# A differential-attention output projection in seven half-sized products, inside a decoder layer

## The chip, the cores and the metric

The kernel runs on one core of a Trainium2 chip, in one launch. The metric is the device time of one execution in microseconds, the median of several runs. All data are float32. The core's engines, as the profile names them: PE is TensorE (matmuls; PEld its weight loads), DVE is VectorE, ACT is ScalarE, POOL is GpSimd, and SP is the engine that only issues transfers here.

## The reference

One decoder layer for 512 tokens of width 1024. One combined input projection feeds three attention branches and three gates; each branch is projected to 1024 columns, the three are merged by sigmoid gates, projected again, added to the residual and normalised. Then follow an MLP of width 4096 with a squared ReLU, a gated per-layer embedding, and a second normalisation.

```python
proj = x @ w_in                                   # 512 x 1024 @ 1024 x 10752
(da_q, da_k, da_v, sb_q, sb_k, sb_v, dl_q, dl_k, dl_v, gates) = split(proj)
o_da = diff_attention(da_q, da_k, da_v, ...)      # 512 x 512, differential
o_sb = stick_breaking_attention(sb_q, sb_k, sb_v) # 512 x 512
o_dl = dilated_attention(dl_q, dl_k, dl_v, ...)   # 512 x 512
g = sigmoid(gates).reshape(B, S, 3, 1024)
merged = (g[:, :, 0] * (o_da @ w_branch_da) + g[:, :, 1] * (o_sb @ w_branch_sb)
          + g[:, :, 2] * (o_dl @ w_branch_dil))
x = layer_norm(alpha * x + merged @ w_out)
hid = relu(x @ w_up)
c = square(hid) @ w_down
ple = sigmoid(x @ w_ple_gate) * (p @ w_ple)
x = layer_norm(alpha * x + c + ple)
```

## The kernel before

Every large matmul is done in three passes. An operand `a` is split into a rounded part `h` (a cast on ScalarE) and a rest `l` (a subtraction on VectorE), and the product is `h*h + h*l + l*h`. Weights come in chunks of 128 x 1024 (512 KB): SP loads a chunk into one of seven raw tiles (`fill`, L182), ScalarE casts it to `wh` (L212), VectorE subtracts to `wl` (L214), and both live in rings of six. `pump` issues these splits as the chunks six places ahead are released.

The kernel is a list of items, executed in order. An item has a `mm` function that issues its matmuls into a PSUM bank (`mm_bank`, two, or `at_bank`, six), an `ev` function that evicts the bank and is issued at the next item, and optionally a `pre` function. Beside the items run generators, advanced by `step()` once or twice an item: the attention heads, and in `pending` other helpers. The tile framework orders the instructions of each engine when the program is built, so an engine's order need not be the source order.

Several products are already done in seven half-sized ones: with both matrices cut in 2 x 2 blocks, seven block products (called 2, 1, 7, 6, 4, 5, 3 in their order) of sums and differences of blocks give what eight would. This is so for the values of the dilated branch, the three gates (`seven`, used by `gate_alone` and `gate_chain`), the gate of the per-layer embedding, and the MLP. Sums of activation blocks (the "forms") are made on VectorE. Sums of weight blocks (`vsum`, `msum`, `gsum`, `usum`, `dsum`) are made by transfers on POOL's queue, from memory to memory with addition (`sum_steps`, L985 and L987): eight steps for each four sums. `credit` in the main loop grows by an item's size times its rate, and a step is issued for each whole unit; each step waits for a recent weight split.

The stages in order: the input projections with the attention heads between them, the stick-breaking branch (`branch_items(1)`), its gate, a second gate, the dilated branch, the third gate, the differential branch (`branch_items(0)`), the output projection (`wout_items`), the per-layer embedding, the MLP, and the last normalisation.

The differential branch before: `split_oT(0)` splits four tiles of 128 x 512 (attention output, transposed). For each half of the 1024 columns and each of four token tiles an item does 4 x 3 matmuls of 128 x 512 (L648 to L650). Its eviction multiplies the gate by the bank (L659) and adds it to `merged` (L660). A gate's sigmoid is made in place ahead of its item (`gate_sig`, L501). Behind each of the last four items stands a `turn_item(k)`: four transposes of 128 x 128 (L676), one column block of `merged` for all 512 tokens, split into `mh` and `ml` (L680, L681). The other four column blocks are turned among the first items of the output projection, whose first column half is therefore cut: all token tiles do the first four blocks of the inner dimension, then all do the last four (L766 to L770, evicted at L784).

Of the kernel before, what the change touches and what calls it, by code (L numbers as in the profile page):

```python
# [18 lines left out]
P = 128  # L19
# [36 lines left out]
def trunk(tc, a, out):  # L56
    nc = tc.nc
    es = ExitStack()
    with es:
# [14 lines left out]
        def slot(name, dt=F32):  # L74
            return big.tile([P, 512], dt, name=nm(name), tag="s", bufs=NSLOT)
# [7 lines left out]
        def at_bank():  # L83
            return psum.tile([P, 512], F32, name=nm("at"), tag="at", bufs=6)
# [67 lines left out]
        def chunk(src, w):  # L152
            return chunk_of(load(src, w))
# [78 lines left out]
        def item(cs, mm, ev, need=None, bank=None, size=1.0):  # L232
            items.append({"c": cs, "mm": mm, "ev": ev, "need": need, "bank": bank, "size": size})
# [403 lines left out]
        def branch_items(i, behind=()):  # L637
            behind = list(behind)
            for half in range(2):
                cs = [chunk(a["wb"][i, half, c].rearrange("p k n -> p (k n)"), 1024) for c in range(2)]  # L640
                for tt in range(4):
                    def mm(ps, tt=tt, cs=cs):
                        q = slice(tt * P, tt * P + P)
                        for k in range(4):
                            c = cs[k // 2]
                            n = slice(k % 2 * 512, k % 2 * 512 + 512)
                            h, lo = oTs[4 * i + k]
                            nc.tensor.matmul(ps, h[:, q], c["h"][:, n], start=k == 0, stop=False)  # L648
                            nc.tensor.matmul(ps, h[:, q], c["l"][:, n], start=False, stop=False)
                            nc.tensor.matmul(ps, lo[:, q], c["h"][:, n], start=False, stop=k == 3)  # L650

                    def ev(ps, tt=tt, half=half):
                        if i == 1:
                            t = slot("b1")
                            nc.scalar.copy(t, ps)
                            merged[tt, half] = t
                            return
                        g = sg.pop((i, tt, half))
                        nc.vector.tensor_mul(g, g, ps)  # L659
                        nc.vector.tensor_add(merged[tt, half], merged[tt, half], g)  # L660
# [7 lines left out]
                    if half and behind:  # L668
                        behind.pop(0)()

        merged_T = {}

        def turn_item(k):
            def mm(ps):
                for tt in range(4):
                    nc.tensor.transpose(ps[:, tt * P:tt * P + P], merged[tt, k // 4][:, k % 4 * P:k % 4 * P + P], ident)  # L676

            def ev(ps):
                h, lo = slot("mh", F32R), slot("ml", F32R)
                nc.scalar.copy(h, ps)  # L680
                nc.vector.tensor_sub(lo, ps, h.bitcast(F32))  # L681
                merged_T[k] = (h, lo)
            item([], mm, ev, size=0.08)

        last_plain = len(items)
        for it in items:
            it.setdefault("rate", 2.5)
        def first_gate(tt, half):
            g = gate_sig(1, tt, half)
            nc.vector.tensor_mul(merged[tt, half], merged[tt, half], g)  # L690
# [5 lines left out]
        for n, i in ((1, 2), (2, 0)):  # L696
            gate_chain(n, i)
            if n == 1:
                for j, th in enumerate([(tt, half) for half in range(2) for tt in range(4)]):
                    items[gated_at + 2 + j]["pre"] = lambda th=th: first_gate(*th)  # L700
            branch_at[i] = len(items)
            branch_items(i, () if i else [lambda k=k: turn_item(k) for k in range(4)])

        raws = {}
        forms = {}
# [46 lines left out]
        ln2_at = [None]  # L752

        def wout_items():
            kept = {}
            for half in range(2):
                cs = [chunk(a["wo"][half, c].rearrange("p k n -> p (k n)"), 1024) for c in range(4)]

                def part(tt, ks, last, half=half, cs=cs):
                    def mm(ps):  # L760
                        for k in ks:
                            c = cs[k // 2]
                            s = slice((k % 2) * 512, (k % 2) * 512 + 512)
                            h, lo = merged_T[k]
                            q = slice(tt * P, tt * P + P)
                            nc.tensor.matmul(ps, h[:, q], c["h"][:, s], start=k == 0, stop=False,  # L766
                                             skip_group_check=True)
                            nc.tensor.matmul(ps, h[:, q], c["l"][:, s], start=False, stop=False,
                                             skip_group_check=True)
                            nc.tensor.matmul(ps, lo[:, q], c["h"][:, s], start=False, stop=k == 7,  # L770
                                             skip_group_check=True)

                    def bank():
                        if ks[0] == 0:
                            kept[tt, half] = at_bank()
                        return kept[tt, half]

                    def ev(ps):
                        if ks[-1] != 7:
                            return  # L780
# [9 lines left out]
                    need = [cs[c] for c in sorted({k // 2 for k in ks})]  # L790
                    item(need if last else [], mm, ev, need=need, bank=bank, size=len(ks) / 8)
                if half:
                    for tt in range(4):
                        part(tt, range(8), tt == 3)
                    continue
                for tt in range(4):
                    part(tt, range(4), tt == 3)
                    for k in {1: (4, 5), 2: (6, 7)}.get(tt, ()):
                        turn_item(k)
                for tt in range(4):  # L800
                    part(tt, range(4, 8), tt == 3)

        def ln1_gen(tt):
            def fin(h, t):
# [153 lines left out]
        def sum_steps():  # L958
# [883 lines left out]
        for n, it in enumerate(items):  # L1842
# [5 lines left out]
                while active or waiting:  # L1848
                    step()
            for i in range(3):  # L1850
                if n == branch_at[i] - 2:
                    while any(k not in ready for k in range(4 * i, 4 * i + 4)):
                        step()
                    split_oT(i)
# [105 lines left out]
def _layout(x, p, w_in, da_lambda, da_norm, w_branch_da, w_branch_sb, w_branch_dil, w_out, ln1_g, ln1_b,  # L1960
# [17 lines left out]
    def quarters(w):  # L1978
# [8 lines left out]
        "wt": c(np.stack(tiles[2:])),  # L1987
        "wv": c(np.stack(vs)),

        "wb": c(np.stack([token_major(w[0]) for w in (w_branch_da, w_branch_sb, w_branch_dil)])),  # L1990
# [34 lines left out]
```

## The time and the profile before

| | |
|---|---|
| runs | 1054.17 us median (1053.24 to 1054.87, three runs) |
| the profiled execution | 1053.95 us, span 1052.0 us |
| granted clock of TensorE | 0.997 |
| gate items' end, differential branch, output projection | 585.4 to 601.7, 601.7 to 625.4, 625.4 to about 670 us of the span |

The span runs from the first to the last instruction of the profiled execution. In a row of a timeline the first number is the start, the second the duration, and the bracket, where there is one, the idle time before it with what ended it. In a row of the groups, the total busy time and the mean duration in ns stand behind the first bar and the idle time before them behind the second. In the table of stretches each engine has its busy time and, behind an x, its instructions.

### The profile page before, as it was taken

What the parts mean: (1) busy time and instruction counts of PE and PEld (TensorE: products, weight loads), DVE (VectorE), ACT (ScalarE), POOL (GpSimd) and SP (SyncE); (2) the same over time, 40 slices, a digit from 0 to 9 for tenths busy, and PEclk for the clock granted to TensorE, in tenths of its full rate; (3) what the DMA queues carried; (4) which work ended last, traced back from release to release, by engine and by line L of the source; (5) the groups of instructions that cost most, each with busy time, mean ns of one, the idle gap of its engine ahead of it and who ended that gap; (6) DMA issues with size and microseconds to landing.
All of it is one profiled execution on the core that took longest, in us unless ns stands there. A gap on an engine that the chain in (4) does not pass through costs nothing.

```text
span 1052.0 us, 15035 instructions
## 1 busy us (share of the span) xinstructions
PE 1037.5 (99%) x5474; PEld 883.7 (84%) x5474; DVE 763.5 (73%) x1356; ACT 582.9 (55%) x990; POOL 177.7 (17%) x271
## 2 busy tenths in 40 slices
PE   9999999999999999999999999999999999999997
PEld 6887788888888887888888888888999889889885
DVE  6888667749864746788666664888778877877966
ACT  6666545526444645667554723675666665566651
POOL 0012401320203322211121240111121111111000
PEclk9999999999999999999999999999999999999998
DMA  8348965995847999547998996269999899998512
GB/s 320 112 162 256 216 199 195 312 277 186 275 115 220 305 283 271 182 173 238 280 340 269 309 333 198 87 208 324 332 327 320 285 289 295 313 277 281 190 35 80
DMA packets 72761, 254.32 MB, mean 242 GB/s; under 512 B 8968, under 2 KB 9880, under 8 KB 72688
## 3 DMA queue, kind: packets, MB, share of 16 engines
q0 software_dynamic: 32464, 116.21, 42.2%
q1 hardware_dynamic: 39648, 136.24, 35.6%
q8 instruction: 43, 0.70, 0.3%
q10 hardware_dynamic: 576, 0.92, 0.2%
q14 instruction: 30, 0.25, 0.1%
HBM read 251.21 MB, written 106.98 MB: 340 GB/s over the span
## 4 chain that ended last, share of the span: by engine, by line
PE 84%; DMA 9%; DVE 3%; ACT 2%; issue 1%; POOL 0%; SPq 0%; DVEq 0%; POOLq 0%; ACTq 0%
PE mm L87 8%; PE mm L89 7%; PE mm L88 7%; PE at L1147 4%; PE at L1148 4%; PE at L1149 4%; DMA msum<-in_wgm_dram 4%; PE at L556 3%; PE at L555 3%; PE at L554 3%; PE mm L453 2%; PE mm L455 2%; PE mm L454 2%; DMA gsum<-gsum 2%; PE at L89 1%; PE at L88 1%
## 5 line engine op out<-in xcount | busy, mean ns | idle before, releaser
L214 DVE TENSOR_TENSOR wl<-raw,wh 128x1024 fp32r<-128x1024 f32 x251 | 305.3, 1222 | 126.6 <-ACT wh L212 124.4
L212 ACT CAST wh<-raw 128x1024 fp32r<-128x1024 f32 x251 | 262.7, 1050 | 234.0 <-PE mm L88 127.1
L87 PE MATMUL mm<-xhT,wh 128*128 128x512 f32 x304 | 121.1, 398 | 0.0
L89 PE MATMUL mm<-xhT,wl 128*128 128x512 f32 x304 | 119.0, 391 | 0.0
L88 PE MATMUL mm<-xlT,wh 128*128 128x512 f32 x304 | 118.8, 391 | 0.0
L1147 PE MATMUL at<-wh,hh 128*128 128x512 f32 x188 | 73.7, 392 | 0.0
L1148 PE MATMUL at<-wl,hh 128*128 128x512 f32 x188 | 73.7, 392 | 0.0
L87 PE MATMUL mm<-x1hT,wh 128*128 128x256 f32 x256 | 73.6, 288 | 0.0
L1149 PE MATMUL at<-wh,hl 128*128 128x512 f32 x188 | 73.1, 389 | 0.0
L88 PE MATMUL mm<-x1lT,wh 128*128 128x256 f32 x256 | 72.3, 283 | 0.0
L89 PE MATMUL mm<-x1hT,wl 128*128 128x256 f32 x256 | 71.8, 283 | 0.0
L89 PEld LDWEIGHTS mm<-xhT,wl 128*128 128x128 f32 x304 | 57.1, 188 | 12.3
L87 PEld LDWEIGHTS mm<-xhT,wh 128*128 128x128 f32 x304 | 57.2, 188 | 11.6 <-issue 0.4
L88 PEld LDWEIGHTS mm<-xlT,wh 128*128 128x128 f32 x304 | 57.2, 188 | 10.4
L87 PEld LDWEIGHTS mm<-x1hT,wh 128*128 128x128 f32 x256 | 48.8, 191 | 4.7 <-ACT up L1081 2.8
L88 PEld LDWEIGHTS mm<-x1lT,wh 128*128 128x128 f32 x256 | 48.8, 191 | 1.5
L89 PEld LDWEIGHTS mm<-x1hT,wl 128*128 128x128 f32 x256 | 48.6, 191 | 0.0
L985 POOL DMA_DIRECT2D usum<-in_wu_dram x32 | 27.6, 879 | 107.6 <-DVE wl L214 75.7
L1149 PEld LDWEIGHTS at<-wh,hl 128*128 128x128 f32 x188 | 35.3, 188 | 7.7
L1147 PEld LDWEIGHTS at<-wh,hh 128*128 128x128 f32 x188 | 35.5, 189 | 6.0
L1148 PEld LDWEIGHTS at<-wl,hh 128*128 128x128 f32 x188 | 35.5, 189 | 5.5
L985 POOL DMA_DIRECT2D dsum<-in_wd_dram x28 | 23.5, 848 | 96.5 <-DVE wl L214 74.7
(563 smaller groups left out, 2662.3 us busy)
## 6 DMA issues: line engine op xcount, KB each, us to landing
usum<-in_wu_dram POOLq DMA_DIRECT2D x48, 512.0 KB, 9.7
dsum<-in_wd_dram POOLq DMA_DIRECT2D x42, 512.0 KB, 9.0
raw<-in_wt_dram SPq DMA_DIRECT2D x38, 512.0 KB, 6.5
msum<-in_wgm_dram POOLq DMA_DIRECT2D x36, 512.0 KB, 12.7
raw<-usum SPq DMA_DIRECT2D x32, 512.0 KB, 8.1
raw<-dsum SPq DMA_DIRECT2D x28, 512.0 KB, 7.3
raw<-in_wd_dram SPq DMA_DIRECT2D x25, 512.0 KB, 5.3
raw<-msum SPq DMA_DIRECT2D x24, 512.0 KB, 6.0
```

What stands on the lines that cost most here:

```text
L87: nc.tensor.matmul(ps, wh, xh, start=start, stop=False, skip_group_check=True)
L88: nc.tensor.matmul(ps, wh, xl, start=False, stop=False, skip_group_check=True)
L89: nc.tensor.matmul(ps, wl, xh, start=False, stop=stop, skip_group_check=True)
L212: i = nc.scalar.copy(h, raw)
L214: i = nc.vector.tensor_sub(lo, raw, h.bitcast(F32))
L554: nc.tensor.matmul(ps, h[:, q], c["h"][:, n], start=go, stop=False, skip_group_check=True)
L555: nc.tensor.matmul(ps, h[:, q], c["l"][:, n], start=False, stop=False, skip_group_check=True)
L556: nc.tensor.matmul(ps, lo[:, q], c["h"][:, n], start=False, stop=end, skip_group_check=True)
L985: i = nc.gpsimd.dma_start(o, i, accum_op=OP.add, max_dma_last_dim=4096)
L1147: nc.tensor.matmul(ps, h[:, q], c["h"][:, s], start=go, stop=False, skip_group_check=True)
L1148: nc.tensor.matmul(ps, h[:, q], c["l"][:, s], start=False, stop=False, skip_group_check=True)
L1149: nc.tensor.matmul(ps, lo[:, q], c["h"][:, s], start=False, stop=end, skip_group_check=True)
```

## The change

The differential branch is computed in seven products as well. The attention output (512 tokens by 512) and `w_branch_da` are cut in 2 x 2 blocks; a product has 256 tokens (two items of 128), an inner dimension of 256 and 512 columns: 2 x 3 matmuls an item.

- `branch_forms` takes the place of `split_oT(0)` and starts six items ahead of the branch instead of two, as a generator with five steps. It makes eight 256-wide sums and seven splits where four splits stood.
- `branch_seven` takes the place of `branch_items(0)`: 14 items of 6 matmuls for 8 of 12. Four of the seven weight operands are sums, from memory (`bsum`, eight more steps in `sum_steps`, in the queue after `msum`). Products 6, 5 and 3 add onto the bank of product 1, product 4 onto that of 7.
- A `turn_item` now has a token half and two column blocks. Four stand behind products 6, 6, 5 and 3; the others stand after the first and the second item of the output projection, which is no longer cut: each of its items does all eight blocks.
- The rates of the sum steps change: 2.6 for 2.5 in the input projections, the branch item's size 0.25, the first output items up to 8 for 12, and 0.58 for 0.56 in the MLP.
- The residual's eight tiles (`load_xn`) are requested eight and four items ahead of the output projection instead of one.

```diff
+        def branch_forms(i):
+            o = [oT.pop(4 * i + k) for k in range(4)]
+            f = slot("o7")
+            fk = [f[:, HB], f[:, HC]]
+            for k in range(2):
+                nc.vector.tensor_sub(fk[k], o[2 + k][:, HC], o[k][:, HC])
+            sp = {k: split(o[k], "oT") for k in (2, 3)}
+            yield
+            for k in range(2):
+                nc.vector.tensor_sub(o[k][:, HC], o[k][:, HB], o[k][:, HC])
+                sp[k] = split(o[k], "oT")
...
+            whole(7)
+            yield
+            for p, k0 in ((6, 0), (4, 2)):
+                for k in range(2):
+                    nc.vector.scalar_tensor_tensor(fk[k], fk[k], -1.0, o[k0 + k][:, HB], op0=OP.mult, op1=OP.subtract)
+                whole(p)
+                yield
...
+        def branch_seven(i, behind):
+            s, b, cs = {}, {}, {}
+            for p in (2, 1, 7, 6, 4, 5, 3):
+                for r in range(2):
+                    if not r:
+                        blk = {1: 0, 2: 1, 4: 3}.get(p)
+                        cs[p] = chunk(bsum[{5: 0, 6: 1, 7: 2, 3: 3}[p]] if blk is None else
+                                      a["wbq"][blk].rearrange("p k n -> p (k n)"), 1024)
...
+                    def ev(ps, p=p, r=r):
+                        if p in (2, 7, 6):
+                            s[p, r] = slot("b0")
+                            nc.scalar.copy(s[p, r], ps)
+                            return
+                        v, to = {1: (2, (r, 0)), 4: (6, (r, 1)), 5: (7, (2 + r, 1)), 3: (None, (2 + r, 0))}[p]
+                        if v is not None:
+                            nc.vector.tensor_add(s[v, r], s[v, r], ps)
+                        g = sg.pop((i, *to))
+                        nc.vector.tensor_mul(g, g, ps if v is None else s[v, r])
+                        m = merged[to]
+                        (nc.vector.tensor_add if p in (1, 3) else nc.vector.tensor_sub)(m, m, g)
+                    item([cs[p]] if r else [], mm, ev, need=[cs[p]], bank=bank, size=0.25)
...
-        def turn_item(k):
+        def turn_item(h, th, kp):
             def mm(ps):
-                for tt in range(4):
-                    nc.tensor.transpose(ps[:, tt * P:tt * P + P], merged[tt, k // 4][:, k % 4 * P:k % 4 * P + P], ident)
+                for k in range(2):
+                    for t in range(2):
+                        o, c = k * 256 + t * P, (2 * kp + k) * P
+                        nc.tensor.transpose(ps[:, o:o + P], merged[2 * th + t, h][:, c:c + P], ident)
...
-            it.setdefault("rate", 2.5)
+            it.setdefault("rate", 2.6)
...
-            branch_items(i, () if i else [lambda k=k: turn_item(k) for k in range(4)])
+            if i:
+                branch_items(i)
+            else:
+                branch_seven(i, {(6, 0): [(0, 0, 0)], (6, 1): [(0, 0, 1)], (5, 1): [(1, 0, 0)], (3, 0): [(1, 0, 1)]})
...
+                    item(cs if tt == 3 else [], mm, ev, need=cs, bank=at_bank)
+                    for t in {0: [(1, 1, 0), (1, 1, 1)], 1: [(0, 1, 0), (0, 1, 1)]}.get(tt, ()) if not half else ():
+                        turn_item(*t)
...
+            todo.append(up_steps(bsum, a["wbq"]))
             todo.extend(up_steps(gsum[m], a["wg"][m]) for m in range(2))
...
-            if 12 <= n < wout_at + 12:
+            if 12 <= n < wout_at + 8:
                 credit += it["size"] * it.get("rate", 1.0)
             elif n > ple_at + 6:
-                credit += 0.56
+                credit += 0.58
...
+            if n == wout_at - 8:
+                load_xn(0)
+            if n == wout_at - 4:
+                load_xn(1)
             if n == wout_at - 1:
-                load_xn(0)
-                load_xn(1)
                 ln_consts("ln1_g", "ln1_b")
```

More of the change, by code (lines that the diff above doesn't have):

```diff
@@ L635, in gate_chain, with branch_items @@
             seven(xf, mixer_operand(n), {"first": (2, 1, 7), "last": (2, 4, 3), "get": get}, done)
-        def branch_items(i, behind=()):
-            behind = list(behind)
+        def branch_items(i):
             for half in range(2):
-                cs = [chunk(a["wb"][i, half, c].rearrange("p k n -> p (k n)"), 1024) for c in range(2)]
+                cs = [chunk(a["wb"][i - 1, half, c].rearrange("p k n -> p (k n)"), 1024) for c in range(2)]
                 for tt in range(4):
@@ L667, in branch_items, with whole @@
                         items[-1]["pre"] = pre
-                    if half and behind:
-                        behind.pop(0)()
+        bsum = [dram.tile([P, 1024], F32, name=f"bsum{i}") for i in range(4)]
+        of = {}
+        def branch_forms(i):
[9 more added lines that the diff above has]
+                sp[k] = split(o[k], "oT")
+            for p, k0, c in ((1, 0, HB), (5, 0, HC), (2, 2, HB), (3, 2, HC)):
+                of[p] = [[t[:, c] for t in sp[k0 + k]] for k in range(2)]
+            yield
+            def whole(p):
+                h, lo = split(f, f"o{p}")
+                of[p] = [(h[:, c], lo[:, c]) for c in (HB, HC)]
+            whole(7)
[4 more added lines that the diff above has]
+                whole(p)
+                yield
@@ new lines, in branch_seven, with bank, mm, pre @@
+        def branch_seven(i, behind):
[6 more added lines that the diff above has]
+                                      a["wbq"][blk].rearrange("p k n -> p (k n)"), 1024)
+                    def bank(p=p, r=r):
+                        name = {1: "x", 6: "x", 5: "x", 3: "x", 7: "y", 4: "y", 2: "z"}[p]
+                        if p in (1, 2, 7):
+                            b[name, r] = at_bank()
+                        return b[name, r]
+                    def mm(ps, p=p, r=r):
+                        q, c = slice(r * P, r * P + P), cs[p]
+                        for k in range(2):
+                            n = slice(k * 512, k * 512 + 512)
+                            h, lo = of[p][k]
+                            go, end = k == 0 and p in (1, 2, 7), k == 1 and p in (2, 3, 4)
+                            nc.tensor.matmul(ps, h[:, q], c["h"][:, n], start=go, stop=False, skip_group_check=True)
+                            nc.tensor.matmul(ps, h[:, q], c["l"][:, n], start=False, stop=False, skip_group_check=True)
+                            nc.tensor.matmul(ps, lo[:, q], c["h"][:, n], start=False, stop=end, skip_group_check=True)
+                    def ev(ps, p=p, r=r):
[11 more added lines that the diff above has]
+                    item([cs[p]] if r else [], mm, ev, need=[cs[p]], bank=bank, size=0.25)
+                    items[-1]["rate"] = 1.5
+                    to = {2: (r, 0), 7: (r, 1), 6: (2 + r, 1), 4: (2 + r, 0)}.get(p)
+                    if to:
+                        def pre(to=to):
+                            sg[(i, *to)] = gate_sig(i, *to)
+                        items[-1]["pre"] = pre
+                    for t in behind.get((p, r), ()):
+                        turn_item(*t)
@@ L671, in trunk @@
         merged_T = {}
-        def turn_item(k):
+        def turn_item(h, th, kp):
             def mm(ps):
-                for tt in range(4):
-                    nc.tensor.transpose(ps[:, tt * P:tt * P + P], merged[tt, k // 4][:, k % 4 * P:k % 4 * P + P], ident)
+                for k in range(2):
+                    for t in range(2):
+                        o, c = k * 256 + t * P, (2 * kp + k) * P
+                        nc.tensor.transpose(ps[:, o:o + P], merged[2 * th + t, h][:, c:c + P], ident)
@@ L678, in ev @@
             def ev(ps):
[L679 to L682, printed above, removed]
+                hi, lo = slot("mh", F32R), slot("ml", F32R)
+                nc.scalar.copy(hi, ps)
+                nc.vector.tensor_sub(lo, ps, hi.bitcast(F32))
+                merged_T[h, th, kp] = (hi, lo)
             item([], mm, ev, size=0.08)
@@ L754, in wout_items, with mm, ev @@
         def wout_items():
-            kept = {}
             for half in range(2):
                 cs = [chunk(a["wo"][half, c].rearrange("p k n -> p (k n)"), 1024) for c in range(4)]
-                def part(tt, ks, last, half=half, cs=cs):
-                    def mm(ps):
-                        for k in ks:
+                for tt in range(4):
+                    def mm(ps, tt=tt, cs=cs):
+                        for k in range(8):
                             c = cs[k // 2]
                             s = slice((k % 2) * 512, (k % 2) * 512 + 512)
[L764 to L780, printed above, removed]
+                            h, lo = merged_T[k // 4, tt // 2, k % 4 // 2]
+                            q = slice(k % 2 * 256 + tt % 2 * P, k % 2 * 256 + tt % 2 * P + P)
+                            nc.tensor.matmul(ps, h[:, q], c["h"][:, s], start=k == 0, stop=False)
+                            nc.tensor.matmul(ps, h[:, q], c["l"][:, s], start=False, stop=False)
+                            nc.tensor.matmul(ps, lo[:, q], c["h"][:, s], start=False, stop=k == 7)
+                    def ev(ps, tt=tt, half=half):
                         y = xn.pop((tt, half))
@@ L789, in ev @@
                             pending.append(ln1_gen(tt))
[L790 to L801, printed above, removed]
+                    item(cs if tt == 3 else [], mm, ev, need=cs, bank=at_bank)
+                    for t in {0: [(1, 1, 0), (1, 1, 1)], 1: [(0, 1, 0), (0, 1, 1)]}.get(tt, ()) if not half else ():
+                        turn_item(*t)
         def ln1_gen(tt):
@@ L1850, in trunk @@
             for i in range(3):
-                if n == branch_at[i] - 2:
+                if n == branch_at[i] - (2 if i else 6):
                     while any(k not in ready for k in range(4 * i, 4 * i + 4)):
                         step()
-                    split_oT(i)
+                    if i:
+                        split_oT(i)
+                    else:
+                        pending.append(branch_forms(i))
             need = it["need"] or it["c"]
@@ L1988, in _layout @@
         "wv": c(np.stack(vs)),
-        "wb": c(np.stack([token_major(w[0]) for w in (w_branch_da, w_branch_sb, w_branch_dil)])),
+        "wb": c(np.stack([token_major(w[0]) for w in (w_branch_sb, w_branch_dil)])),
+        "wbq": c(w_branch_da[0].reshape(2, 2, 128, 2, 512).transpose(3, 0, 2, 1, 4).reshape(4, 128, 2, 512)),
         "wgm": c(np.stack([quarters(w_in[:, OFF["gate"] + 1024 * i:OFF["gate"] + 1024 * i + 1024]) for i in (1, 2, 0)])),
```

## The prediction

> **What bounds the kernel now.** I read the busy shares first, then the slices, then TensorE's own waits.
>
> ```profile
> span 1052.0 us, 15035 instructions
> PE 1037.5 (99%) x5474; PEld 883.7 (84%) x5474; DVE 763.5 (73%) x1356; ACT 582.9 (55%) x990; POOL 177.7 (17%) x271
> ...
> PE   9999999999999999999999999999999999999997
> ```
>
> TensorE is busy for 1037.5 of 1052.0 us and no slice but the last falls below nine tenths. What is left is the start and the tail. The waits of TensorE:
>
> ```profile
> PE at L1325 <- DVE zero L1322: 1.3, 1, 1.3
> PE mm L648 <- DVE da_klb L101: 1.1, 1, 1.1
> ```
>
> These two are the longest of nine such groups. So the order written in the kernel hides everything else, and a matmul removed anywhere is worth its slot, as long as no new wait opens. The timeline of TensorE at the start of the differential branch gives that slot:
>
> ```profile
> 601.73 0.39 PE L648 MATMUL at<-wh,oTh 128*128 128x512 f32 x1
> ...
> 604.45 0.39 PE L648 MATMUL at<-wh,oTh 128*128 128x512 f32 x1
> ```
>
> From 601.73 to 604.45 run the 12 matmuls of one branch item: 2.72 us, or 0.2267 us each. The duration of 0.39 us overlaps with the next matmul; it is not the price. Priced by duration, 12 matmuls would be 4.7 us. The Trainium skill (Trainium Kernel Development and Optimization, Performance Expectations) says that matmul busy time is a bad metric because matmuls are pipelined; this trace agrees, with a start every 0.23 us under a duration of 0.39.
>
> **The matmuls.** Before: two halves of columns, four token tiles, 4 x 3 matmuls each, 96. After: seven products, two token tiles each, 2 x 3 matmuls, 84. All are 128x512 as before. Removed: 12 x 0.2267 = **2.72 us**. The output projection keeps 8 x 24 matmuls, and the transposes stay 8 groups of four, four of them inside the branch and two pairs behind it.
>
> ```profile
> core 0: us, PE busy (x) PEld busy (x) DVE busy (x) ACT busy (x) POOL busy (x), PEclk, DMA share, GB/s
> 585.40:601.70 16.30, 16.30 (x73) 13.52 (x72) 12.00 (x15) 12.33 (x17) 3.75 (x6) 1.00 1.03 312
> 601.70:625.40 23.70, 23.70 (x113) 19.36 (x112) 16.40 (x22) 7.24 (x10) 7.81 (x13) 1.00 1.04 328
> 625.40:670.00 44.60, 44.60 (x211) 36.97 (x210) 25.23 (x47) 15.12 (x27) 6.95 (x12) 1.00 0.51 168
> ```
>
> These are the last six gate items, the branch, and the output projection, all with a full TensorE at clock 1.00. The branch takes 23.7 us: 96 x 0.2267 = 21.8 and 0.5 for each of four transpose groups. It should become 19.0 + 2.0 = 21.0.
>
> **What VectorE gets.** Rows by group, then one stretch of VectorE in the branch:
>
> ```profile
> L214 DVE TENSOR_TENSOR wl<-raw,wh 128x1024 fp32r<-128x1024 f32 x251 | 305.3, 1222 | 126.6 <-ACT wh L212 124.4
> L212 ACT CAST wh<-raw 128x1024 fp32r<-128x1024 f32 x251 | 262.7, 1050 | 234.0 <-PE mm L88 127.1 <-PE at L650 25.1 <-PE at L1149 17.4
> L660 DVE TENSOR_TENSOR b<-b,graw 128x512 f32<-128x512 f32 x16 | 11.0, 690 | 0.4
> L238 DVE TENSOR_TENSOR oTl<-oT,oTh 128x512 fp32r<-128x512 f32 x12 | 7.8, 684 | 0.0
> L1087 DVE TENSOR_TENSOR hid<-mm,up 128x256 f32<-128x256 f32 x16 | 6.8, 422 | 7.9 <-PE mm L89 7.9
> ```
>
> ```profile
> 554.44 1.22 DVE L214 TENSOR_TENSOR wl<-raw,wh 128x1024 fp32r<-128x1024 f32 x1
> 555.57 0.69 DVE L660 TENSOR_TENSOR b<-b,graw 128x512 f32<-128x512 f32 x1
> 556.18 0.68 DVE L659 TENSOR_TENSOR graw<-graw,at 128x512 f32<-128x512 f32 x1
> 556.89 0.69 DVE L660 TENSOR_TENSOR b<-b,graw 128x512 f32<-128x512 f32 x1
> ```
>
> Back to back, a weight split costs VectorE 1.13 us, a 512-wide operation 0.61 to 0.71, say 0.66. The evictions of the seven products are 3 operations for each half of products 1, 4 and 5 and 2 for product 3: 22, where 16 stood. Splits go from 4 to 7, since seven chunks are consumed in the branch and each frees a ring place for the next. With four subtractions of the transposed rows that is 7 x 1.13 + 22 x 0.66 + 4 x 0.66 = **25.1 us of VectorE beside 21.0 us of TensorE**; by the mean durations 8.6 + 15.2 + 2.8 = 26.5. In the gate items just ahead, the forms add eight 256-wide operations (8 x 0.42 = 3.4) and three splits (3 x 0.68 = 2.1): 12.0 + 5.5 = 17.5 beside 16.3 us. So VectorE runs 4 to 7 us behind at the end of the branch. Behind it lie 44.6 us of projection with VectorE busy for 25.2, so the work gets done; the question is only who waits for it meanwhile. ScalarE gains three casts, three splits and six copies: even at 1.05 us for each of the twelve that is 12.6, on 12.33 + 7.24 busy in 40.0 us. It is not near its bound.
>
> Three readers could wait. (a) Products 6, 5 and 3 add onto product 1's bank, so each needs the eviction before it. Two items and a turn or more lie between; for product 3 only one item of 1.36 us and a turn. (b) The turn for the second column half of the first tokens stands behind product 5 and needs product 4's subtraction. TensorE gets there after 12 x 1.36 + 2 x 0.5 = 17.3 us; VectorE has by then 12 evictions, 2 subtractions and 6 splits before it, 14 x 0.66 + 6.8 = 16.0, and starts up to 2.7 us late: a wait of 0 to 1.4 us. (c) The projection of the first tokens reads those turned rows only after 12 matmuls, 2.7 us, on others.
>
> What covers them is that the engine's order need not be the source order:
>
> ```profile
> 615.41 0.69 DVE L660 TENSOR_TENSOR b<-b,graw 128x512 f32<-128x512 f32 x1
> ...
> 615.34 0.49 PE L676 MATMUL mm<-ident,b 128*128 128x128 f32 x3
> 615.58 0.48 PE L648 MATMUL at<-wh,oTh 128*128 128x512 f32 x1
> 615.90 0.40 PE L649 MATMUL at<-wl,oTh 128*128 128x512 f32 x1
> 616.15 0.33 PE L676 MATMUL mm<-ident,b 128*128 128x128 f32 x1
> ...
> 618.63 0.60 PE L676 MATMUL mm<-ident,b 128*128 128x128 f32 x4
> 618.99 0.48 PE L648 MATMUL at<-wh,oTh 128*128 128x512 f32 x1
> ```
>
> The fourth transpose, whose row VectorE finishes at 616.10, was put behind two matmuls of the next item when the program was ordered. In the new order there is more to put forward: products still to come, and 24 matmuls (5.4 us) of the first two projection tiles that need only the first column half. I take the cost of VectorE's lag as 0, because here the same kind of late add cost nothing; the upper bound is the whole lag, 7 us, if nothing is put forward. Below zero it can't go: no wait stands in this stage that could vanish. The Trainium skill (TensorE: Matmul & The Clock Gate, What happens when you issue a matmul) speaks against the cover: on the chip matmuls stay in program order, and only weight loads are pulled ahead. By it a wrong guess in the ordering costs the wait in full; the trace shows an order chosen beforehand, and not what a missed one costs.
>
> **Transfers.**
>
> ```profile
> 571.63 9.89 SPq L182 DMA_DIRECT2D raw<-in_wb_dram  x4
> 582.56 20.68 SPq L182 DMA_DIRECT2D raw<-in_wo_dram  x8
> ...
> raw<-in_wb_dram SPq DMA_DIRECT2D x12, 512.0 KB, 8.4
> ...
> xn<-in_xn_dram POOLq DMA_DIRECT2D x8, 256.0 KB, 9.9
> ```
>
> Three more chunk loads stand ahead of the output weights on SP's queue, in a stage whose DMA share is 1.03. The branch weights are requested 20 to 30 us before 601.73 and land in 8.4, so cost 0; if the lead were gone, 3 x 0.5 MB at 312 GB/s is 5 us. The eight loads of x are moved forward on POOL's queue, past the sum steps there; the rows are first needed after the first projection tile, and land in 9.9 us: 0 either way, the sum steps behind them lose about 8 x 0.54 us of issue.
>
> The eight steps for the new sums are queued on POOL before those of the later weights. Counting the credits of every item, 140 steps are issued before the per-layer embedding now; after, 142 of which 8 are new, so the MLP's sums run six steps late, and with 0.58 for 0.56 the last one comes six items later; at 2.72 us an item, 16 us.
>
> ```profile
> 937.75 0.83 POOL L985 DMA_DIRECT2D dsum<-in_wd_dram  x1 [6.10 <-DMA dsum<-dsum]
> ...
> 953.35 0.81 POOL L985 DMA_DIRECT2D dsum<-in_wd_dram  x1 [6.86 <-DMA dsum<-dsum]
> ...
> 961.86 2.21 SPq L182 DMA_DIRECT2D raw<-dsum  x2
> ...
> 997.50 6.88 SPq L182 DMA_DIRECT2D raw<-dsum  x2
> dsum<-in_wd_dram POOLq DMA_DIRECT2D x42, 512.0 KB, 9.0
> ```
>
> The tightest is the second sum of the last block: finished by the step of 937.75, landed by 947, read at 961.86 to 964. Sixteen us later it lands as it is read. The raw ring holds seven chunks, so I take 0; if the delay is a third longer, SP waits 5 us and TensorE at most as long.
>
> **The sum.** The profiled execution took 1053.95 us (span 1052.0 and 1.95 around it). 1053.95 - 2.72 = 1051.23. It lies 0.22 below the median of the runs, 1054.17, so against that 1051.45: forecast **1051.4**.
>
> **Rivals.** (1) *VectorE becomes the bound of the branch* and TensorE waits at the turns and at product 3. The rows give 4.1 to 7 us of lag; if it is paid in full the net is +1.4 to +4.3, **1055.3 to 1058.2**, middle 1056.8, slower by more than 0.2% (2.1 us, about what a measurement can tell here) once TensorE loses over 4.8. For it: 25.1 against 21.0, and readers one item away. Against: filler matmuls, and 16.4 of 23.7 us of VectorE now without a wait. (2) *Half of it*: 0.6 to 4.8 us are lost, middle 2.5, result **1053.7**, within 0.2%. (3) *The denser sums of the projections* (2.6 for 2.5) put two more steps ahead of the x loads of the value forms:
>
> ```profile
> 177.24 7.85 DMA msum<-msum
> ...
> 222.80 11.12 DMA xr<-in_xT_dram
> ...
> L420 PE MATMUL mm<-wh,u7h x4: 387/390/505, 250.1 to 256.6; 128*128 128x512 f32 x4
> L238 DVE TENSOR_TENSOR u7l<-fr,u7h x2: 690/691/692, 236.4 to 237.2; 128x512 fp32r<-128x512 f32 x2
> ```
>
> The form ends at 237.9 and is used at 250.1: 12.2 us of room. Two steps one after the other at the 7.85 us of a step in this chain are 15.7, and they mostly overlap; if they don't, 3.5 us are lost: **1054.7**. (4) *Late MLP sums* cost their 5 us: **1056.2**. (5) *The change does not shorten TensorE* would show as 5474 matmuls again; the loops count 84, so I give it no chance.
>
> **Chances.** Forecast, gain over 2.1 us: 0.54. Within 0.2%: 0.26 (rival 2 with 0.23, rival 3 with 0.03). Slower by over 0.2%: 0.20 (rival 1 with 0.16, rival 4 with 0.04). The likeliest case's own range is 1050.1 (four transpose groups at the 0.36 us from 618.63 to 618.99 instead of 0.5, and the 0.8 us by which the runs lie from their median) to 1052.1. The whole reaches from there to 1056.8, the middle of rival 1, which leaves out about one in ten above and less below.
>
> **What would show it.** Right: 5462 matmuls, TensorE full in all slices, the branch 21 us long, VectorE at nine tenths in it, its last subtraction 4 to 7 us after the branch's last matmul, and projection matmuls standing among those of products 5 and 3. Wrong: waits of TensorE on the merged rows, on the transposed halves or on product 5's eviction, worth over 0.6 us together; a shift of the waits near 250 us; SP waiting for sums near 960 us.

## The result

| kernel | runs, median | ratio to the kernel before, 95% interval |
|---|---|---|
| before (the four runs beside it) | 1053.70 us (1052.05 to 1054.87) | 1 |
| changed | 1064.17 us (1063.27 to 1065.05) | 1.0101 [1.0086, 1.0116] |

The change costs 10.5 us; the time lies 12.8 us above the forecast and outside the range. The profiled execution of the changed kernel took 1063.71 us, span 1061.8. Its busy shares and TensorE's slices:

```profile
span 1061.8 us, 15061 instructions
PE 1039.9 (98%) x5462; PEld 884.9 (83%) x5462; DVE 773.6 (73%) x1376; ACT 589.7 (56%) x1002; POOL 182.1 (17%) x279
...
PE   9999999998999998999999999999999999999996
```

The 12 matmuls are gone (5462 for 5474), and yet TensorE is busy for 2.4 us longer. Two slices have lost their nine: the tenth and the sixteenth of 26.5 us each, near 240 and near 410 us. Both lie far ahead of the branch, which runs from 611 us. TensorE's waits name the two places:

```profile
PE at L1778 <- DVE r L1771: 4.1, 1, 4.1
PE mm L420 <- ACT dl_q L285: 3.6, 1, 3.6
PE at L1385 <- DVE zero L1382: 1.3, 1, 1.3
PE mm L647 <- DVE da_klb L101: 1.1, 1, 1.1
...
PE at L844 <- ACT mh L757: 0.2, 1, 0.2
```

The first two are new at this size. Before, the same list had these:

```profile
PE at L1718 <- DVE r L1711: 0.6, 1, 0.6
...
PE mm L420 <- ACT dl_q L285: 0.2, 1, 0.2
```

The 0.6 us for `r` belong to another head, at 251 us; the matmul that now waits 4.1 us did not wait at all. The last line of the changed kernel's list is all that the new branch and the projection made TensorE wait. A table of the same matmuls in both traces shows where the time went (starts, in us):

| matmul | before | changed | shift |
|---|---|---|---|
| last value product (u5h) | 277.5 | 280.8 | +3.3 |
| first of the stick-breaking branch | 432.0 | 443.6 | +11.6 |
| last of the third gate's product 4 (u4h) | 590.2 | 601.7 | +11.5 |
| last of the output projection | 671.2 | 680.7 | +9.5 |
| last of the down projection's L1147, L1207 | 1037.7 | 1047.2 | +9.5 |

So: a first loss of 3.3 us, a second of 8.3, a gain of 2.0 between the third gate and the projection's end, and no shift from there to the last of the down projection.

**The second loss.** GpSimd, VectorE and TensorE around 409 us, changed kernel. L1704 is the power -0.5 in the norm of a differential head; it runs on GpSimd, on the same queue as the sum steps (L1044, L1046).

```profile
403.99 0.52 POOL L1046 DMA_DIRECT2D gsum<-gsum  x1 [2.15 <-DMA gsum<-in_wg_dram]
407.79 0.52 POOL L1046 DMA_DIRECT2D usum<-usum  x1 [3.28 <-DMA usum<-in_wu_dram]
409.09 0.83 POOL L1044 DMA_DIRECT2D bsum<-in_wbq_dram  x1 [0.79 <-DMA bsum<-bsum]
409.66 1.32 POOL L1704 TENSOR_TENSOR ms<-ms,mhalf 128x4 f32<-128x4 f32 x1
411.02 0.16 DVE L1705 TENSOR_TENSOR ms<-ms,rr 128x4 f32<-128x4 f32 x1 [9.87 <-POOL ms L1704]
411.10 0.18 DVE L1771 TENSOR_TENSOR r<-st,exf 128x32 f32<-128x32 f32 x1
411.43 0.60 PE L1778 MATMUL at<-r,fold 128*128 128x32 f32 x2 [4.14 <-DVE r L1771]
```

Read it backwards: TensorE waits for `r`, which takes VectorE 0.18 us but stands behind `ms` on VectorE's queue. VectorE sits idle for 9.87 us in front of `ms`, because GpSimd does the power only after two more sum steps, and each of these waits for a transfer (3.28 and 0.79 us). The same place before:

```profile
400.21 0.53 POOL L987 DMA_DIRECT2D gsum<-gsum  x1 [2.41 <-DMA gsum<-in_wg_dram]
400.76 1.05 POOL L1644 TENSOR_TENSOR ms<-ms,mhalf 128x4 f32<-128x4 f32 x1
401.85 0.16 DVE L1645 TENSOR_TENSOR ms<-ms,rr 128x4 f32<-128x4 f32 x1 [3.95 <-POOL ms L1644]
```

There the power stood right behind the second step on `gsum`, and VectorE's idle time of 3.95 us was just short enough.

**The first loss.** The value forms and ScalarE, changed kernel:

```profile
233.24 0.54 POOL L347 DMA_DIRECT2D xr<-in_xT_dram  x1 [3.03 <-DMA msum<-in_wgm_dram]
237.89 0.62 ACT L237 CAST u7h<-fr 128x512 fp32r<-128x512 f32 x1 [8.62 <-DVE fr L370]
239.76 0.62 ACT L237 CAST u7h<-fr 128x512 fp32r<-128x512 f32 x1 [1.26 <-DVE fr L370]
241.35 0.60 ACT L285 ACTIVATE dl_q<-mm 128x512 f32<-128x512 f32 x1
242.00 0.62 PE L420 MATMUL mm<-wh,xhT 128*128 128x512 f32 x1 [3.63 <-ACT dl_q L285]
```

The same places before:

```profile
229.11 0.54 POOL L347 DMA_DIRECT2D xr<-in_xT_dram  x1 [3.07 <-PE at L1571]
234.66 0.62 ACT L237 CAST u7h<-fr 128x512 fp32r<-128x512 f32 x1 [5.14 <-DVE fr L370]
238.13 0.60 ACT L285 ACTIVATE dl_q<-mm 128x512 f32<-128x512 f32 x1
```

The last load of x leaves GpSimd's queue at 233.24, for 229.11 before: in GpSimd's timeline 47 sum steps stand ahead of the first load of x, for 45 before. The form made from the loads is late, ScalarE waits 8.62 us for it, for 5.14 before, and behind that cast on ScalarE's queue stands the copy `dl_q`, 3.2 us later than before, which frees the bank that TensorE wants.

### The profile page after: what moved, and what is told of

It reads as the page before. It is cut to its first block, busy times and chain, and to the rows that moved or that the text cites. A ratio compares the mean times of both kernels' runs of the same rounds, so it can differ in the third digit from the quotient of the medians.

```text
span 1061.8 us, 15061 instructions
## 1 busy us (share of the span) xinstructions
PE 1039.9 (98%) x5462; PEld 884.9 (83%) x5462; DVE 773.6 (73%) x1376; ACT 589.7 (56%) x1002; POOL 182.1 (17%) x279
## 4 chain that ended last, share of the span: by engine, by line
PE 81%; DMA 11%; issue 4%; DVE 2%; ACT 1%; POOL 0%; SPq 0%; DVEq 0%; POOLq 0%; ACTq 0%
PE mm L87 8%; PE mm L88 7%; PE mm L89 7%; DMA msum<-in_wgm_dram 4%; PE at L1207 4%; PE at L1208 4%; PE at L1209 4%; DMA bsum<-bsum 3%; PE at L554 3%; PE at L556 3%; PE at L555 3%; DMA gsum<-in_wg_dram 1%; PE at L89 1%; PE at L88 1%; PE at L87 1%
## 5 line engine op out<-in xcount | busy, mean ns | idle before, releaser
L214 DVE TENSOR_TENSOR wl<-raw,wh 128x1024 fp32r<-128x1024 f32 x254 | 308.9, 1222 | 124.6 <-ACT wh L212 122.4
L212 ACT CAST wh<-raw 128x1024 fp32r<-128x1024 f32 x254 | 265.9, 1050 | 234.6 <-PE mm L88 129.5
L1207 PE MATMUL at<-wh,hh 128*128 128x512 f32 x188 | 73.7, 392 | 0.0
L1044 POOL DMA_DIRECT2D usum<-in_wu_dram x32 | 27.0, 871 | 112.9 <-DVE wl L214 84.2
L1044 POOL DMA_DIRECT2D dsum<-in_wd_dram x28 | 24.0, 878 | 101.9 <-DVE wl L214 68.0
L1207 PEld LDWEIGHTS at<-wh,hh 128*128 128x128 f32 x188 | 35.5, 189 | 6.0
```

The source lines that it names most:

```text
L212: i = nc.scalar.copy(h, raw)
L214: i = nc.vector.tensor_sub(lo, raw, h.bitcast(F32))
L1044: i = nc.gpsimd.dma_start(o, i, accum_op=OP.add, max_dma_last_dim=4096)
L1207: nc.tensor.matmul(ps, h[:, q], c["h"][:, s], start=go, stop=False, skip_group_check=True)
```

## Experiments

Theory A: the rate of the sum steps in the projections, 2.6 for 2.5, makes both losses. Its rival, theory B: the rate makes the first loss, and the eight new steps, put into GpSimd's queue, make the second. The third is the prediction's own rival, VectorE as the bound of the branch.

**1. The changed kernel at the old rate.**

```diff
-            it.setdefault("rate", 2.6)
+            it.setdefault("rate", 2.5)
...
-                credit += 0.58
+                credit += 0.61
```

> The changed kernel with the rate of the sum steps in the projections put back from 2.6 to 2.5, and 0.61 for 0.58 in the MLP so that the sums still end in time; the seven products, their sums and everything else stay. Theory A (the denser steps make both losses: they stand on POOL's queue ahead of the eight loads of x near 220 us and ahead of the power of the head's norm near 409 us): both losses of 3.3 and 8.2 us go and the branch's gain of about 2.0 stays, so 1054 - 2 = about 1052. Theory B (the rate makes only the first loss; the eight steps of the new sums, put into the queue ahead of the gate's, make the second): only 3.3 goes, about 1061. The prediction's rival 1 (VectorE bounds the branch): no less than 1055, with waits of TensorE between 601 and 630 us.

Measured: 1052.46 us, ratio 0.9996 [0.9981, 1.0012]; profiled span 1050.1. Both long waits are gone, `dl_q` altogether and `r` is back at 0.6 us. Theory A, and no room for rival 1. In the trace the kernel is 1.9 us shorter than before (span), in the medians 0.75, which cannot be told from no change: its twelve runs spread from 1050.1 to 1055.4.

**2. The old kernel at the new rate.**

```diff
-            it.setdefault("rate", 2.5)
+            it.setdefault("rate", 2.6)
```

> The kernel before with one number changed: 2.6 for 2.5 as the rate of the sum steps in the projections. No seven products, no new sums. Theory A: the two losses come without the branch's change, about 3.3 + 8.2 = 11.5 us, so 1065; waits of TensorE of about 4 us near 242 and near 411 us. Theory B: the first loss alone, about 1057. If the losses belong to neither (the new stage's own doing): 1054.

Measured: 1066.95 us, 1.0134 [1.0121, 1.0147]. One number, without any of the new products, makes the kernel slower than the whole change does. Its waits of TensorE:

```profile
PE at L1718 <- DVE r L1711: 4.9, 1, 4.9
PE mm L420 <- ACT dl_q L285: 4.4, 1, 4.4
```

**3. No new sum steps, new rate.**

```diff
-                        cs[p] = chunk(bsum[{5: 0, 6: 1, 7: 2, 3: 3}[p]] if blk is None else
-                                      a["wbq"][blk].rearrange("p k n -> p (k n)"), 1024)
+                        blk = {5: 0, 6: 1, 7: 2, 3: 3}[p] if blk is None else blk
+                        cs[p] = chunk(a["wbq"][blk].rearrange("p k n -> p (k n)"), 1024)
...
-            todo.append(up_steps(bsum, a["wbq"]))
```

> The changed kernel without the eight transfers that add up the weights of the branch; products 5, 6, 7 and 3 read plain blocks of the weight instead (so this kernel leaves out the weight sums of the branch). The rate stays 2.6. Theory A: other sum steps move up into the places of the eight, the queue in front of the loads of x and of the norm's power is as long as before, and both losses stay: 1062 to 1065. Theory B: the second loss goes, 1056.

Measured: 1065.32 us, 1.0117 [1.0104, 1.0130], with waits of 4.9 (`r`) and 3.8 us (`dl_q`). The kernel leaves out the weight sums of the branch, so it computes another result, and only its time is read here. Theory B falls: one of the two steps ahead of the power in the changed kernel is a new one (`bsum`), but without the new ones two steps on `usum` and one on `gsum` stand there. What counts is how many steps stand in front, not whose they are.

**4. The power off GpSimd's queue.**

```diff
-                nc.gpsimd.tensor_tensor(ss, ss, mhalf.to_broadcast([P, 4]), OP.pow)
+                nc.scalar.activation(ss, ss, AF.Ln)
+                nc.scalar.activation(ss, ss, AF.Exp, scale=-0.5)
```

> The changed kernel with one thing moved off POOL's queue: the power -0.5 of the norm of a differential head is done on ScalarE, as a logarithm and an exponential of -0.5 of it. Both theories have the same cause for the second loss (VectorE waits for that power, which waits in POOL's queue behind sum steps): the wait of 4.1 us of TensorE near 411 us and the slow matmuls behind it go, 8.2 us less, 1056; the first loss of 3.3 us stays. If the loss near 411 us comes from the transfers themselves or from the clock alone: 1064 as after. ScalarE may lose a little to the two more instructions of each of eight heads, some 8 x 2 x 0.2 us that nobody waits for.

Measured: 1055.26 us, 1.0025 [1.0016, 1.0035], 8.9 less than the changed kernel (8.3 in the spans of the profiled executions). In its timeline the sum steps are as late as ever, and nobody waits for them:

```profile
402.06 0.20 ACT L1704 ACTIVATE ms<-ms 128x4 f32<-128x4 f32 x1 [2.03 <-DVE ms L1703]
404.30 0.16 DVE L1706 TENSOR_TENSOR ms<-ms,rr 128x4 f32<-128x4 f32 x1
...
409.59 0.52 POOL L1046 DMA_DIRECT2D usum<-usum  x1 [2.67 <-DMA usum<-in_wu_dram]
```

**5. The loads of x earlier.** The eight loads of `value_forms` become a function of their own:

```diff
+            if n == v_from[0] - 3:
+                load_values()
             if n == v_from[0]:
                 pending.append(value_forms())
```

> The changed kernel, rate 2.6, with the eight loads of x for the value forms requested three items earlier, so that they stand ahead of more of the sum steps on POOL's queue; the forms themselves stay where they are. If the first loss (the late u7h cast standing ahead of the dl_q cast on ScalarE) comes from the late loads: TensorE's wait of 3.6 us near 242 us goes and the second loss stays, 1064.2 - 3.3 = about 1061 (up to 1060, if the slow matmuls behind the wait cost more than the landmarks show). If the loads are late for another reason (DMA engines): 1064.

Measured: 1058.70 us, 1.0046 [1.0028, 1.0064]. The wait for `dl_q` is gone, the one for `r` stays at 4.5 us. The gain is 5.5 us where 3.3 was expected: the table of matmuls compares with a kernel that itself lost time here, as experiment 6 shows.

**6. Both moves, in the changed kernel and in the one before.** The diffs of 4 and 5 together, the rate at 2.6 in the first and 2.5 in the second.

> The changed kernel, rate 2.6, with both: the loads of x three items earlier and the norm's power on ScalarE. If the two queue places make the whole loss: the two waits of about 4 us go, and the time is the kernel before less the branch's gain of 2.0, so 1051.7; a little less if the shorter waits of the kernel before near 242 and 411 us (0.2, 0.6 and 1.0) go too, about 1050. Rival 1 of the prediction (VectorE bounds the branch): no less than 1055.

> The kernel before (rate 2.5, no seven products in the branch) with the same two moves, as the measure for the run above: what the branch's change is worth with neither wait in the way is the difference of the two. If the moves only take away waits that the denser steps bring: 1053 to 1053.7, and 1.5 to 2 us above the run above. If the moves are good by themselves (the waits of 0.2, 0.6 and 1.0): 1051.5 to 1052.5. If the branch's change is worth its forecast 2.72: that much above the run above.

Measured: the changed kernel with both 1048.88 us, 0.9952 [0.9936, 0.9968]; the kernel before with both 1050.64 us, 0.9968 [0.9957, 0.9979]. The page of the changed one:

```profile
span 1047.1 us, 15069 instructions
PE 1033.8 (99%) x5462; PEld 881.6 (84%) x5462; DVE 774.3 (74%) x1376; ACT 594.3 (57%) x1013; POOL 178.0 (17%) x275
...
PE   9999999999999999999999999999999999999996
```

It is faster than the kernel before, at the very rate that made the change slow. The kernel before gains 2.4 us from the two moves in the medians, and 3.4 in the rows of the profiled executions: its last u5h goes from 277.5 to 275.4, its first stick-breaking matmul from 432.0 to 428.6. It had been paying a little at both places all along. Both kernels with the moves reach the last u4h matmul at the same 586.8 us, so from there on they show the branch by itself. The last matmul of the projection starts at 667.8 without the seven products and at 665.9 with them: the change is worth **1.9 us** (medians: 1.8).

**7. The wait filled with work.** In front of L1778, in the last dilated head:

```diff
-            px = at_bank()
+            px = at_bank(); [nc.tensor.matmul(px, k[0][:, 0:P], q[0], start=True, stop=True, skip_group_check=True) for _ in range(18 if hd == 3 else 0)]
```

> The changed kernel with 18 matmuls of 128x512, whose results nobody reads, in front of the matmul that waits near 411 us (18 x 0.2267 = 4.08 us, the length of the wait): TensorE has work while the wait lasts and the wait itself stays as long. If the half clock behind the idle stretch makes half of the loss: no half clock behind it, about 1064.2 - 4 = 1060. If the loss of 8.2 us has another source than the clock (the late VectorE, late buffers): 1064.

Measured: 1069.73 us, 1.0147 [1.0127, 1.0167]. The fill was mis-sized. These operands are plain f32, and the 18 matmuls show as 36 records over 15.5 us, not 4.1. TensorE's timeline, then the table of stretches (busy time and instructions of each engine, granted clock, DMA share, GB/s):

```profile
409.31 15.61 PE L1777 MATMUL at<-dl_q,dl_k 128*128 128x512 f32 x36
424.76 0.30 PE L1778 MATMUL at<-r,fold 128*128 128x32 f32 x2
```

```profile
core 0: us, PE busy (x) PEld busy (x) DVE busy (x) ACT busy (x) POOL busy (x), PEclk, DMA share, GB/s
409.30:424.80 15.50, 15.50 (x39) 6.87 (x37) 5.84 (x24) 4.09 (x11) 5.98 (x8) 1.00 1.01 252
424.80:434.00 9.20, 9.20 (x53) 7.58 (x52) 7.94 (x26) 5.14 (x10) 0.00 (x0) 1.00 0.55 170
```

The fill outlasts the wait, so this run can't tell the clock from a late VectorE, as it was meant to: no matmul on `r` waits behind the fill, whatever held it. What it does show is that nothing more is lost behind a pause that is filled. From the last u5h to the first stick-breaking matmul the kernels without the wait for `r` take 153.2 us (experiments 4 and 6), the changed one 162.8, this one 167.4 (450.3 less 282.9). So 15.5 us of useless matmuls cost 14.2, no more than their own length, and the granted clock behind them is 1.00.

The rows of the changed kernel decide between the two. In it TensorE sat idle for 5.2 us (4.14, and 1.05 for a second `r`) and lost 9.6. The stretch behind the wait has a granted clock of 0.50, and its timeline shows the spacing:

```profile
411.43:421.02 9.59, 8.54 (x21) 6.44 (x22) 6.20 (x28) 4.09 (x11) 3.13 (x5) 0.50 1.01 194
```

```profile
412.42 0.63 PE L88 MATMUL mm<-xlT,wh 128*128 128x512 f32 x1
412.85 0.63 PE L89 MATMUL mm<-xhT,wl 128*128 128x512 f32 x1
...
420.67 0.52 PE L88 MATMUL mm<-xlT,wh 128*128 128x512 f32 x1
421.02 0.39 PE L89 MATMUL mm<-xhT,wl 128*128 128x512 f32 x1
421.25 0.39 PE L87 MATMUL mm<-xhT,wh 128*128 128x512 f32 x1
```

Starts lie 0.43 us apart instead of 0.23; 17 such matmuls from 411.85 to 420.67 are 3.4 us. The first and the last of this stretch in the kernel with both moves (L1783 there is L1778 here):

```profile
401.87 0.31 PE L1783 MATMUL at<-r,fold 128*128 128x32 f32 x2
...
406.19 0.39 PE L89 MATMUL mm<-xhT,wl 128*128 128x512 f32 x1
```

The same matmuls take 4.32 us there, and 9.59 here (411.43 to 421.02): 5.27 more. Of these 1.05 are the second pause, and 4.2 are slower starts with no wait in front of them. With the pause of 4.14 that makes the 9.6, to 0.2 us: what was lost beyond the idle time is the half clock, not a late VectorE.

**8. The missing 0.8 us of the gain.** Projection items of the second token half take the column blocks in another order; the run of both moves is repeated beside it.

```diff
-                        for k in range(8):
+                        ks = [*range(8)] if tt < 2 else [4, 5, 6, 7, 0, 1, 2, 3]
+                        for k in ks:
...
```

> As the changed kernel with both moves (loads of x earlier, norm's power on ScalarE), and in the output projection the items of the second token half take the column blocks 4 to 7 first and 0 to 3 last, since the transposed blocks 0 to 3 of that half are the last to be ready. If the missing 0.8 us of the branch's gain (1.9 for the forecast 2.72) lie in the last group of transposes and its wait on ScalarE's cast, which stretch from 631.58 to 632.85 in that kernel: the wait of 0.24 us goes and up to 0.5 us with it, 1048.4 to 1048.6. If the group is late for its own sake (the two banks, VectorE's last subtraction): same as the run beside it.

> The changed kernel with both moves once more, on the same chip as the run above, as its measure: 1048.9 as before, and 4 us below the kernel before.

Measured: 1048.49 us, 0.9961 [0.9948, 0.9974], and 1049.18 us, 0.9969 [0.9958, 0.9979] for the repeat. Their intervals against the kernel before overlap, but five of the six runs lie below all eleven of the repeat, and the rows show where. TensorE's timeline with both moves, and then with the swapped order:

```profile
631.58 1.03 PE L757 MATMUL mm<-ident,b 128*128 128x128 f32 x8
632.85 0.50 PE L848 MATMUL at<-wh,mh 128*128 128x512 f32 x1 [0.24 <-ACT mh L761]
```

```profile
632.37 1.03 PE L757 MATMUL mm<-ident,b 128*128 128x128 f32 x8
633.16 0.48 PE L849 MATMUL at<-wh,mh 128*128 128x512 f32 x1
```

The group of eight transposes took 1.27 us up to the next matmul, and takes 0.79. From the last u4h to the projection's last matmul it is 78.5 us, for 79.0 in the repeat. This kernel has the lowest median of the study.

## Why the prediction was wrong

**The matmuls, right in kind.** 84 for 96, full clock, no wait worth the name. Forecast 2.72 us, measured 1.9 with the other losses out of the way. Of the 0.8 between, 0.5 stood in the last transposes, which the prediction had counted as unchanged because their number was (experiment 8). The rest wasn't tested.

**VectorE, right.** It is busy for nine tenths of the branch, and its last subtraction follows the branch's last matmul by 4 to 5 us, in the stretches and in the timeline of the changed kernel:

```profile
610.80:637.80 27.00, 27.00 (x128) 22.04 (x127) 24.30 (x35) 16.53 (x24) 8.14 (x14) 1.00 1.03 310
```

```profile
638.22 0.39 PE L722 MATMUL at<-wh,oTl 128*128 128x512 f32 x1
642.46 0.69 DVE L735 TENSOR_TENSOR b<-b,graw 128x512 f32<-128x512 f32 x1
```

Projection matmuls were put among those of the last products, as expected, so the branch takes 27 us with others' work in it, where 21 were forecast for its own, and TensorE stays full. The lag cost at most the 0.5 us of experiment 8, of which 0.2 are the wait for `mh`. Rival 1, with its 0.16, had no part in the result.

**Transfers and late MLP sums, right.** From the projection's last matmul to that of L1147 and L1207 it is 366.5 us in both kernels.

**The denser steps, wrong.** This is the step that failed: rival 3, priced at 3.5 us and given a chance of 0.03, and so a term put at nothing in the sum. What came was a first loss of 3.3 us and a second of 8.3. The two more steps ahead of the loads of x were counted rightly, and a shift of the waits near 250 us was named as a sign of being wrong; it came. Three things were wrong with the step:

- *The room.* The 12.2 us were measured from the end of u7l to the matmul that uses it. But a late form delays whatever stands behind its cast on ScalarE, and that was `dl_q`. The wait list of before already had TensorE waiting for `dl_q`, 0.2 us: the room was nothing.
- *The queue.* The prediction went through SP's queue and through the loads of x on GpSimd's, but did not look for instructions that are not transfers there. The norm's power is one, with VectorE idle for 3.95 us in front of `ms` in the trace of before. This loss, the larger, was in no rival.
- *The price.* A wait was priced at its length. The second loss took 9.6 us for 5.2 idle (8.3 against the kernel before, whose own stretch is 1.3 longer than without any wait there). The Trainium skill (TensorE: Matmul & The Clock Gate, What happens when you issue a matmul) says that matmuls stay in program order, from which the prediction concluded that a late one costs its wait in full; the trace agrees as far as it goes, since TensorE did nothing else during the 4.14 us, and the price was higher still.

All of it hung on one number of the diff, 2.6 for 2.5, which the prediction followed only to the MLP's sums and the loads of x.

## What to carry to other kernels

When a change puts more issues on a queue, or the same ones earlier, list every instruction on that queue behind them, compute ones too, and for each who waits for it: slack is read at the nearest blocked queue, not at the operand's use. Where TensorE is full, an existing wait of a few tenths in the wait list means that the margin is spent. The pauses of TensorE of some 4 us cost 1.3 to 1.9 times the idle time here (7.5 us for 5.7 and 9.6 for 5.2, at the same place). The two remedies (another engine for a tiny operation, a load three items earlier) were worth about as much in the kernel before as the twelve matmuls: 2.4 us for 1.8 in the medians.

## What the runs showed of the hardware

After the idle 4.14 us of the changed kernel TensorE ran at half clock for some 9 us, with a second pause of 1.05 us among them. After 4.5 us at the same place in experiment 5, from 402.2 to 406.6, the half clock ended earlier. The table of stretches of that kernel has, for the 9.4 us behind the pause, a granted clock of 0.82 where the changed kernel has 0.50:

```profile
406.63:416.00 9.37, 8.16 (x31) 6.27 (x32) 6.21 (x28) 4.70 (x12) 3.15 (x5) 0.82 0.99 190
```

So the same wait cost 7.5 us in the one profile (160.7 us for the stretch that takes 153.2 without it) and 9.6 in the other. The Trainium skill (TensorE: Matmul & The Clock Gate, What's actually happening) has the clock at half after an idle window of about 3.4 us and at full after a busy one of the same length, in windows that run freely. The half clock after some 4 us agrees, and so do the starts 0.43 us apart for 0.23. The 9 us do not speak against it: the matmuls ahead of the second pause filled only 3.3 us (411.43 to 414.76), and behind it, from 415.80 on, the clock was full again after some 5 us, more than one such window and less than two.

The half clock did not always begin with the end of a pause. Behind the idle 3.63 us of the first loss, five matmuls still start 0.23 to 0.24 us apart (242.46 to 243.40), and only from 243.79 on do the starts lie 0.43 apart. That stretch too cost more than its idle time: the last u5h starts at 280.8 in the changed kernel and at 275.5 with both moves, 5.3 us for 3.63 idle.
